# Filler streams that stop at a mark, and transposes that are issued later, in a two-block transformer kernel

## The chip, the cores and the metric

The kernel runs on one core of a Trainium2 chip. The metric is the device time of one execution in microseconds (us), lower is better. One profiled execution gives a trace: every instruction of TensorE (PE; its weight loads, which overlap the products, are PEld), VectorE (DVE), ScalarE (ACT) and GpSimd (POOL), and the transfers (DMA), with start, length and what it waited for.

## The reference

Two blocks of two layers each run on 256 tokens of width 1024, in fp32. Cut to the order of the steps:

```
# first block (h: 256 x 1024)
for i in 0, 1:
    u = rms_norm(h);  y = stick_breaking_attention(u) if i == 0 else dilated_attention(u)
    h += rms_norm(y); u = rms_norm(h)
    h += rms_norm(square(relu(u @ w_ff_in[i])) @ w_ff_out[i])
    h += (p[i] @ w_ple[i]) * sigmoid(rms_norm(h) @ w_ple_gate[i])
# second block: x = h and a context xc of 256 more tokens; shift, scale, gate from a small product
for i in 0, 1:
    hl, hc = modulate(x), modulate(xc)
    oc, ol = mla_pool_mixer(hc, hl) if i == 0 else gqa_mixer(hc, hl)   # layer 1: keys and values of xc only
    x += gate * ol;  x += gate * conv_ffn(modulate(x))
    if i == 0: xc += gate * oc;  xc += gate * conv_ffn(modulate(xc))
return rms_norm(x) * g_final
```

dilated_attention projects to q, k and v of 3 groups of heads, turns q and k by rope, and takes a softmax over masked scores. mla_pool_mixer has low-rank q and k/v paths (cq, ck) and a pooling branch with a product after it. conv_ffn is up, a convolution over three tokens, silu times u, down.

## The kernel before

**Products.** All products keep fp32 accuracy by splitting an operand in a rounded half and its remainder: `mm3` (lines 194 to 197) issues three products for one. A weight block of 512 KB is brought into a stage `ws`, ACT casts it to `wh` (L183) and DVE subtracts that to get `wl` (L184); `put_split` (L200, L201) does the same for activations. Inputs of a product must lie with the feature on the partitions, so normalised tokens go through TensorE transposes (`flip_group`, L231), and heads through others (L786, L813, L833, L837 in the dilated attention, L965 in `heads_T`, L1355 in the gqa mixer). PSUM tiles come from three pools of two buffers each: `acc` (two banks a tile), `mm` (the main path) and `fx` (fillers).

**Stages.** In the profiled execution the stick-breaking attention ends at about 175 us, the first FFN with its ple step at about 475, the dilated attention at about 690, the second FFN and ple at about 960, the latent MLA mixer at about 1130, the first conv FFN at about 1390, the gqa mixer at about 1500, and the last conv FFN at the end.

**Fillers.** The context xc needs nothing of the first block. Its work is a Python generator, `ctx_gen` then `ctx1_gen`, in the queue `ctx`: a norm (`ctx_norm`), `mla_gen` on the context (also used for the latent with main-path tiles), the out projection, a second `ctx_norm`, the context's conv FFN, a third `ctx_norm`. The main path calls `fill(n)` where TensorE would wait: the call adds n to the queue's credit and steps the generator while credit is left. A step yields its price in us of TensorE (negative while it holds open PSUM banks). In the dilated attention, `proj(qr + 1)` is stepped in the same way (queue `main`) between the steps of `attend(qr)`; for the last one, qr = 3, no projection is left and the queue `ctx` fills (`ctx_ok`). The `FILL` table holds the credits. `until_dense(n)` steps the queue until a long product stream lies ahead.

**Order.** These generators set in which order instructions are written. A scheduler then orders each engine's row by its own estimates, and each engine runs its row strictly in order. SyncE issues the weight transfers in its own row.

Of the kernel before, what the change touches and what calls it, by code (L numbers as in the profile page):

```python
# [14 lines left out]
ALU = mybir.AluOpType  # L15
# [4 lines left out]
D = 1024  # L20
# [8 lines left out]
PBUFS = 4  # L29
FILL = dict(sb1=5.0, sb2=1.25, sb3=0.5, sb_end=6.0, sbd=6.0, sbm=0.8, m0=1.0, mix0=8.5, mix1=8.5, f1c=1.6,  # L30
            f1d=8.0, post0=9.6, post1=12.0, dp0=5.6, dp1=8.0, ple0=10.0, ple1=10.0, dl0=3.38, dl1=7.65, dl2=2.4,
# [70 lines left out]
def two_block_kernel(ctx: ExitStack, tc: tile.TileContext, a: dict, out: bass.AP, dbg=None):  # L102
# [139 lines left out]
    def norm_one(src, g, shift, f, tt, bank):  # L242
# [5 lines left out]
        for grp in f.groups:  # L248
# [8 lines left out]
            c0 += w  # L257

    class Feat:

# [54 lines left out]
    dense = [0.0]  # L315

    def fill_step(q):
        try:
            w = next(queues[q][0])
            open_banks[q] = w < 0  # L320
            credit[q] -= abs(w)
        except StopIteration:
            open_banks[q] = False
            queues[q].pop(0)
            if q == "mod":
                credit[q] = 0.0

    def clean(q):
# [3 lines left out]
    def fill(n, q="ctx"):  # L332
        if q in rival:
            clean(rival[q])
        credit[q] += n
        while credit[q] > 0 and queues[q]:
            fill_step(q)
        if not queues[q]:
            credit[q] = 0.0
# [307 lines left out]
    def ffn1(i, u, before_end):  # L647
        w1, w2 = a["w_ff_in"][i], a["w_ff_out"][i]
        G = FF1 // 256
        with tc.tile_pool(name="ff", bufs=2) as p:  # L650
# [35 lines left out]
            for g in range(G):  # L686
                if g + 1 < G:
                    up(g + 1)
                next(gv, None)
                if i == 1:  # L690
                    pass
                elif g < G - 3:
                    fill(FILL["f1c"])
                elif g == G - 3:
                    until_dense(FILL["f1d"])
                if g == G - 2:
                    clean("ctx")
                    for _ in gv:
                        pass
                    before_end()  # L700
                down(g)
                if i == 1:
                    next(gv, None)
        return y

# [39 lines left out]
    def dilated(u):  # L745
        w_in, w_out = a["w_in_dil"][0], a["w_out_dil"][0]
        wv = w_in.rearrange("k (g r n) -> k g r n", g=3, r=3)
        with tc.tile_pool(name="dl", bufs=2) as p:
# [3 lines left out]
            def proj(qr):  # L752
                v = p.tile([128, 2, 3, 128], F32, tag="v", name="v")
                qk = p.tile([128, 3, 512], F32, tag="qk", name="qk")
                for g in range(3):
# [12 lines left out]
                    tok = p.tile([128, 2, 4, 64], F32, tag="tok", name="tok")  # L768
                    for tt in range(2):
# [11 lines left out]
                    vec.tensor_tensor(out=x2, in0=x2, in1=r[1], op=ALU.add)  # L781
                    ps = mm1()
                    for part in range(2):
                        for tt in range(2):
                            c0 = part * 256 + tt * 128
                            pe.transpose(ps[:, c0:c0 + 128],  # L786
                                         tok[:, tt, 2 * part:2 * part + 2, :].rearrange("p n d -> p (n d)"), ident)
# [136 lines left out]
    def mla_gen(u, rope, p, alloc, bank, pair, score_pair, res, prev):  # L924
# [8 lines left out]
        cq = Feat(alloc, 3, "cq")  # L933
        ps = yield from lin_part(u, KC, mla_w["mix0_w_in"], 0, 384, pair)
        for tt in range(2):
            r = rstd(ps[tt][:, 0:384], 384)
            t = tmp((128, 384))
            vec.scalar_tensor_tensor(out=t, in0=ps[tt][:, 0:384], scalar=r, in1=gq, op0=ALU.mult, op1=ALU.mult)
            to_T(t, cq, tt, bank)
        yield 0.01  # L940
        ck = Feat(alloc, 2, "ck", paired=True)
        kr = p.tile([128, 2, 32], F32, tag="kr", name="kr", bufs=1)
        ps = yield from lin_part(u, KC, mla_w["mix0_w_in"], 384, 288, pair)
        for tt in range(2):
            act.copy(out=kr[:, tt, :], in_=ps[tt][:, 256:288])
            r = rstd(ps[tt][:, 0:256], 256)
            t = tmp((128, 256))
            vec.scalar_tensor_tensor(out=t, in0=ps[tt][:, 0:256], scalar=r, in1=gkv, op0=ALU.mult, op1=ALU.mult)
            to_T(t, ck, tt, bank)
            if rope:  # L950
                rope_pairs(kr[:, tt:tt + 1, :], 1, 16, ca_t[:, tt, :], sa_t[:, tt, :], p)
        yield 0.01
        ps = yield from lin_part(u, KC, mla_w["mix0_w_in"], 672, 512, pair)
# [66 lines left out]
        for g2 in range(2):  # L1020
# [10 lines left out]
            dT = tmp((128, 512))  # L1031
            act.copy(out=dT, in_=ps1)
            ps2 = bank()
            for g in range(2):
                pe.matmul(ps2[:, g * 256:(g + 1) * 256], pws[:, 2 * g2 + g, :], dT[:, g * 256:(g + 1) * 256],
                          start=True, stop=True)
            for g in range(2):
# [4 lines left out]
                cat.put(4 + gg, t)  # L1042
            yield 2.7

# [9 lines left out]
    def soft_heads(nh, nk, q, k, v, dv, scale, dst, p, al, bank, score_pair):  # L1054
# [43 lines left out]
        for hd in range(nh):  # L1098
# [7 lines left out]
            flip(hd)  # L1106
            yield 0.5 * nk
            if (hd + 1) % per == 0:
# [80 lines left out]
    def ctx_norm(k, i, m):  # L1189
        g, sft = mod_row(i, 1, m + 1), mod_row(i, 1, m)  # L1190
        u = Feat(c4, KC, "uc")
        for tt in range(2):
            t = c4([128, D], F32, "xc")
            nc.sync.dma_start(out=t, in_=xc_source(k)[tt * 128:(tt + 1) * 128, :])
            norm_one(t, g, sft, u, tt, fx1)
        return u

    def ctx_gen():
        u = ctx_norm(0, 0, 0)
        yield 4.0  # L1200
        res = {}
# [6 lines left out]
        for nh in range(2):  # L1208
            ps = yield from lin_part(cat, 8, mla_w["mix0_w_out"], nh * 512, 512, fx_pair)
            for tt in range(2):  # L1210
# [6 lines left out]
                nc.sync.dma_start(out=xc_d[0][tt * 128:(tt + 1) * 128, sl], in_=t2)  # L1217
        u = ctx_norm(1, 0, 3)
        yield 4.0
        f = [c4([128, D], F32, "fsum") for _ in range(2)]  # L1220
# [74 lines left out]
    def gqa_kv_gen(u, rope, p, al, bank, pair, res):  # L1295
# [6 lines left out]
        for tt in range(2):  # L1302
# [4 lines left out]
            else:  # L1307
# [3 lines left out]
                              op=ALU.mult)  # L1311
        yield 0.01
        ps1 = bank()
# [10 lines left out]
    def ctx1_gen():  # L1324
        u = ctx_norm(2, 1, 0)
        yield 4.0
        stage_done["ctx1n"] = True
        yield from gqa_kv_gen(u, False, fillp, c4, fx1, fx_pair, gctx)

    def gqa(u):  # L1330
        w_in, w_out = a["gqa_w_in_2"][0], a["gqa_w_out_2"][0]
        with tc.tile_pool(name="gq", bufs=2) as p:
# [9 lines left out]
            def proj(hf, pair, bank):  # L1342
# [8 lines left out]
                yield 0.01  # L1351
                for tt in range(2):
# [152 lines left out]
```

## Time and profile before

| | |
|---|---|
| median of 3 runs | 1722.03 us (1718.5 to 1724.54) |
| the profiled execution | 1722.1 us; its span 1720.3 us; granted TensorE clock 0.988 of full |
| TensorE busy | 1635.5 us, 95% of the span, 10259 matmul instructions |
| VectorE, ScalarE busy | 1211.1 us (70%), 926.6 us (54%) |
| DMA | 337.65 MB, 196 GB/s on average |

The span is the trace from first to last instruction; 1.8 us of the time lie outside of it. Matmuls are pipelined: the length of one includes its fill, and the distance of two starts is what a product costs in a stream.

### The profile page before, as it was taken

Reading aid. Unit: us, or ns where it says so; the run is one execution under the profiler, and the core shown is the slowest. Engines: PE = TensorE matmul, PEld = TensorE weight load, DVE = VectorE, ACT = ScalarE, POOL = GpSimd, SP = SyncE. Lnnn points to the kernel's source line nnn. Section 1 sums busy time; section 2 is a strip of 40 time slices with the busy share of each in tenths; the row PEclk is TensorE's granted clock in tenths of the full one; section 3 lists DMA queues with packets and bytes.
Section 4 is the critical chain, followed back from the end, with each engine's and each line's share of the span. In section 5 each row is a group of like instructions: output and inputs, shape, how many; then the busy total and the mean of one; then the engine's idle time right before and its main releaser. Section 6 shows DMA issues by size and latency. Waiting matters only on the chain.

```text
span 1720.3 us, 28310 instructions
## 1 busy us (share of the span) xinstructions
PE 1635.5 (95%) x10259; PEld 1428.7 (83%) x10260; DVE 1211.1 (70%) x2251; ACT 926.6 (54%) x1854; POOL 44.6 (3%) x69
## 2 busy tenths in 40 slices
PE   7998999999999999989989999999999999989997
PEld 6767888887788879877978898888989987779997
DVE  4437777678788886767767866867686687676665
ACT  5536555545655556544446555764555555545554
POOL 0000000000000000000000000000000000000000
PEclk9999999999999999999999999999999999989999
DMA  7777666665766665777876555345776664246662
GB/s 240 259 257 232 203 217 214 207 217 165 241 186 205 185 188 160 242 236 245 280 231 208 176 172 174 115 136 180 233 239 205 185 187 148 72 153 187 186 187 98
DMA packets 301039, 337.65 MB, mean 196 GB/s; under 512 B 18384, under 2 KB 246164, under 8 KB 300900
## 3 DMA queue, kind: packets, MB, share of 16 engines
q1 hardware_dynamic: 300900, 335.86, 62.4%
q8 instruction: 80, 1.31, 0.3%
q14 instruction: 59, 0.48, 0.1%
HBM read 332.56 MB, written 3.23 MB: 195 GB/s over the span
## 4 chain that ended last, share of the span: by engine, by line
PE 55%; DVE 14%; DMA 13%; issue 4%; ACT 3%; SPq 1%; POOL 1%; ACTq 0%; POOLq 0%; DVEq 0%
PE mm L195 6%; PE mm L196 6%; PE mm L197 6%; PE acc L197 6%; PE acc L196 6%; PE acc L195 6%; DMA ws<-in_w_mod 6%; DVE wl L184 5%; PE fx L195 4%; PE fx L196 4%; PE fx L197 4%; DMA ws<-in_w_ff_in 2%; DVE ga L497 2%; DMA ws<-in_w_in_dil 2%; ACT wh L183 1%
## 5 line engine op out<-in xcount | busy, mean ns | idle before, releaser
L184 DVE TENSOR_TENSOR wl<-ws,wh 128x512 fp32r<-128x512 f32 (+1 forms) x1004 | 638.1, 668 | 273.3 <-ACT wh L183 261.5
L183 ACT CAST wh<-ws 128x512 fp32r<-128x512 f32 (+1 forms) x1004 | 568.6, 604 | 477.8 <-PE mm L196 132.7
L197 PE MATMUL mm<-uh,wl 128*128 128x256 f32 x1344 | 382.9, 285 | 8.4 <-DVE wl L184 8.1
L195 PE MATMUL mm<-uh,wh 128*128 128x256 f32 x1344 | 382.3, 284 | 0.3
L196 PE MATMUL mm<-ul,wh 128*128 128x256 f32 x1344 | 381.5, 284 | 0.0
L197 PEld LDWEIGHTS mm<-uh,wl 128*128 128x128 f32 x1344 | 258.6, 192 | 11.5 <-DVE wl L184 11.0
L195 PEld LDWEIGHTS mm<-uh,wh 128*128 128x128 f32 x1344 | 258.7, 193 | 5.0 <-DVE ul L201 0.9
L196 PEld LDWEIGHTS mm<-ul,wh 128*128 128x128 f32 x1344 | 258.7, 193 | 2.6
L195 PE MATMUL acc<-wh,hh 128*128 128x512 f32 x432 | 172.1, 399 | 0.0
L196 PE MATMUL acc<-wl,hh 128*128 128x512 f32 x432 | 171.3, 397 | 0.0
L197 PE MATMUL acc<-wh,hl 128*128 128x512 f32 x432 | 170.2, 394 | 0.0
L497 DVE SCALAR_TENSOR_TENSOR ga<-ws,cst,ga 128x1024 f32<-128x1024 f32 x84 | 106.3, 1281 | 57.7 <-DMA ws<-in_w_mod 57.5
L195 PE MATMUL fx<-uch,wh 128*128 128x256 f32 x352 | 102.2, 290 | 0.0
L197 PE MATMUL fx<-uch,wl 128*128 128x256 f32 x352 | 100.9, 287 | 0.0
L196 PE MATMUL fx<-ucl,wh 128*128 128x256 f32 x352 | 100.5, 286 | 0.0
L197 PEld LDWEIGHTS acc<-wh,hl 128*128 128x128 f32 x432 | 81.9, 190 | 18.9 <-issue 1.2
L195 PEld LDWEIGHTS acc<-wh,hh 128*128 128x128 f32 x432 | 82.2, 190 | 17.6 <-issue 1.6
L196 PEld LDWEIGHTS acc<-wl,hh 128*128 128x128 f32 x432 | 82.3, 191 | 14.5
L195 PE MATMUL mm<-wh,uh 128*128 128x384 f32 (+1 forms) x256 | 85.3, 333 | 1.9 <-ACT wh L183 1.1
L196 PE MATMUL mm<-wl,uh 128*128 128x384 f32 (+1 forms) x256 | 83.0, 324 | 0.3 <-DVE wl L184 0.3
L197 PE MATMUL mm<-wh,ul 128*128 128x384 f32 (+1 forms) x256 | 82.0, 322 | 0.0
L217 POOL TENSOR_TENSOR s<-s,neghalf 128x1 f32<-128x1 f32 (+2 forms) x52 | 39.9, 767 | 1452.9 <-DVE s L215 1413.1
(405 smaller groups left out, 2705.8 us busy)
## 6 DMA issues: line engine op xcount, KB each, us to landing
ws<-in_ffn_w_up SPq DMA_DIRECT2D x528, 128.0 KB
ws<-in_w_mod SPq DMA_DIRECT2D x96, 512.0 KB
ws<-in_ffn_w_down SPq DMA_DIRECT2D x66, 512.0 KB
ws<-in_w_ff_in SPq DMA_DIRECT2D x64, 512.0 KB
ws<-in_w_ff_out SPq DMA_DIRECT2D x64, 512.0 KB
ws<-in_w_in_dil SPq DMA_DIRECT2D x96, 192.0 KB
ws<-in_w_in_sb SPq DMA_DIRECT2D x24, 512.0 KB
row<-mod SPq DMA_DIRECT2D x19, 512.0 KB
```

The source lines that it names most:

```text
L183: act.copy(out=h[:, s], in_=st[:, s])
L184: vec.tensor_sub(out=l[:, s], in0=st[:, s], in1=f32(h[:, s]))
L195: pe.matmul(o, lh, rh, start=start, stop=False)
L196: pe.matmul(o, lh, rl, start=False, stop=False)
L197: pe.matmul(o, ll, rh, start=False, stop=stop)
L217: gp.tensor_tensor(out=r, in0=v, in1=neghalf.to_broadcast([128, w]), op=ALU.pow)
L497: vec.scalar_tensor_tensor(out=o, in0=st, scalar=c, in1=o, op0=ALU.mult, op1=ALU.add)
```

## The change

A step of a generator can now yield a `Pause`, which is a number like the others; where `fill` meets one, it drops the credit that is left, so that the rest of this call issues nothing more from that queue. Steps whose next instruction needs the result of another engine yield one. The norm of the context becomes a generator too (`norm_tok` works in place at full width, where `norm_one` went by halves). In `mla_gen` the norms of cq and ck are made for both token tiles ahead of the Pause, and the transposes follow it. The product after the pooling (L1035) and the head transposes (L965) get a Pause ahead of them. In the dilated projection the q/k transposes of a group of heads are issued by `flip` after the second weight block of the next group, and use an `fx` bank. In the gqa mixer the k/v stream goes to its Pause first, then the q stream, and both are then drained. In the first FFN the fill of 1.6 per group becomes two of 0.8.

```
-            f1c=1.6,
+            f1c=0.8,
...
+    def norm_tok(t, g, shift):
+        r = rstd(t, D)
+        vec.tensor_mul(out=t, in0=t, in1=g)
+        vec.scalar_tensor_tensor(out=t, in0=t, scalar=r, in1=shift, op0=ALU.mult, op1=ALU.add)
...
+    class Pause(float):
+        pass
     def fill_step(q):
+        w = 0.0
...
+        return isinstance(w, Pause)
...
         while credit[q] > 0 and queues[q]:
-            fill_step(q)
+            if fill_step(q):
+                credit[q] = min(credit[q], 0.0)
...
                 down(g)
                 if i == 1:
                     next(gv, None)
+                elif g < G - 3:
+                    fill(FILL["f1c"])
...  # dilated, proj
                         yield -1.95
+                        if kb == 1 and g - 1 in toks:
+                            flip(g - 1)
+                            yield -0.45
...
-                    ps = mm1()
-                    for part in range(2): ...
-                    act.copy(out=qk[:, g, :], in_=ps)
-                    yield 0.5
+                    toks[g] = tok
+                    yield Pause(0.05)
+                flip(2)
                 keep[qr] = (v, qk)
+                yield 0.5
...  # mla_gen, cq (ck alike)
         for tt in range(2):
             r = rstd(ps[tt][:, 0:384], 384)
-            t = tmp((128, 384))
-            vec.scalar_tensor_tensor(out=t, ...)
-            to_T(t, cq, tt, bank)
-        yield 0.01
+            vec.scalar_tensor_tensor(out=ct[:, tt], ...)
+        yield Pause(2.0)
+        for tt in range(2):
+            to_T(ct[:, tt], cq, tt, bank)
+        yield Pause(1.0)
...
+            yield Pause(1.0)
             heads_T([qtok[:, 0], qtok[:, 1]], qT[hf], act)
-            yield 1.0
+            yield Pause(1.0)
...
             act.copy(out=dT, in_=ps1)
+            yield Pause(1.5)
             ps2 = bank()
...
-            yield 2.7
+            yield Pause(1.2)
...  # soft_heads
-            yield 0.5 * nk
+            yield Pause(0.5 * nk)
...  # ctx_norm
-            norm_one(t, g, sft, u, tt, fx1)
+            norm_tok(t, g, sft)
+            yield Pause(0.1)
+            to_T(t, u, tt, fx1)
+            yield Pause(2.0)
...  # ctx_gen (three places)
-        u = ctx_norm(0, 0, 0)
-        yield 4.0
+        u = yield from ctx_norm(0, 0, 0)
...  # gqa: two steps before transposes yield Pause(0.01) for 0.01, and
-            queues["main"].extend([g0, kvg])
-            while lat.get("kT") is None:
-                fill_step("main")
+            for g in (kvg, g0):
+                while not isinstance(next(g), Pause):
+                    pass
+            queues["main"].extend([kvg, g0])
             drain_main()
```

How the rows of TensorE move is seen at three places. Beside the first FFN, the context's pooling: its first product (L1029, after the change L1059) and the second one (L1035, after L1066), which reads `t`, ACT's copy of the first one's result. `acc<-wh,hh` are the FFN's down products, `mm<-uh,wh` its up products. Before:

```order
L1029 MATMUL fx<-ws,pt 128x256 x4
L195 MATMUL acc<-wh,hh 128x512
L196 MATMUL acc<-wl,hh 128x512
L197 MATMUL acc<-wh,hl 128x512
L195 MATMUL acc<-wh,hh 128x512
L1035 MATMUL fx<-t_3482,ws 128x256 x2
```

After (the lines left out are 64 more of the FFN's products):

```order
L1059 MATMUL fx<-ws,pt 128x256 x4
L195 MATMUL mm<-uh,wh 128x256
L196 MATMUL mm<-ul,wh 128x256
L197 MATMUL mm<-uh,wl 128x256
...
L196 MATMUL acc<-wl,hh 128x512
L197 MATMUL acc<-wh,hl 128x512
L195 MATMUL acc<-wh,hh 128x512
L196 MATMUL acc<-wl,hh 128x512
L197 MATMUL acc<-wh,hl 128x512
L1066 MATMUL fx<-t_3631,ws 128x256 x2
```

Four products stood between the two, and now 72 do.

In the dilated attention, the transposes of a projected group (tok) at one of twelve places. `mm<-wh,uh 128x384` are the projection's products; L833 and L837 (after: L858 and L862) are transposes of the softmax. Before, the group's transposes stand ahead of the next group's first product:

```order
L818 MATMUL acc<-dm_96,ident_b 128x256
L833 MATMUL fx<-ident,P 128x128 x3
L837 MATMUL fx<-ident,P 128x128 x3
L786 MATMUL mm<-ident,tok 128x128 x4
L195 MATMUL mm<-wh,uh 128x384
L196 MATMUL mm<-wl,uh 128x384
```

After:

```order
L858 MATMUL fx<-ident,P 128x128 x3
L862 MATMUL fx<-ident,P 128x128 x3
L195 MATMUL mm<-wh,uh 128x384
L196 MATMUL mm<-wl,uh 128x384
L197 MATMUL mm<-wh,ul 128x384
L195 MATMUL mm<-wh,uh 128x384
L777 MATMUL fx<-ident,tok 128x128 x4
L196 MATMUL mm<-wl,uh 128x384
```

They now stand inside the products of the next group.

In the last dilated attention (qr = 3): `acc<-qk` are scores, `mm<-ident,P` transposes of probabilities, `mm<-PT,v` the products with v, `fx<-uch,wh` products of the context stream, `fx<-ident,xc` its norm's transposes. Before, the piece from the end of the first scores to the second scores:

```order
L802 MATMUL acc<-qk 128x128 x2
...
L196 MATMUL fx<-ucl,wh 128x256
L197 MATMUL fx<-uch,wl 128x256
L813 MATMUL mm<-ident,P 128x128 x3
L195 MATMUL fx<-uch,wh 128x256
L196 MATMUL fx<-ucl,wh 128x256
...
L818 MATMUL acc<-dm_96,ident_b 128x256
L822 MATMUL acc<-qk 128x256 x3
```

After, from the end of the first scores to the products of the context:

```order
L827 MATMUL acc<-qk 128x128 x2
L231 MATMUL fx<-ident,xc 128x128 x8
L847 MATMUL acc<-qk 128x256
L838 MATMUL mm<-ident,P 128x128 x3
...
L847 MATMUL acc<-qk 128x256 x3
L838 MATMUL mm<-ident,P 128x128 x3
L858 MATMUL mm<-ident,P 128x128 x3
L862 MATMUL mm<-ident,P 128x128 x3
...
L874 MATMUL mm<-PT_6756,v 64x256
...
L231 MATMUL fx<-ident,xc 128x128 x8
L195 MATMUL fx<-uch,wh 128x256
```

Before, context products stand between the steps of this attention; after, the only context work inside it is one group of 8 transposes, and 144 context products come behind it and behind a second group. On VectorE the norm of that second group stands behind the last copy of the attention's probabilities (`PT`):

```order
L757 TENSOR_SCALAR P<-P,s 128x768
L859 COPY PT_6757<-mm 128x3x128
L215 TENSOR_SCALAR s<-s 128x1
L262 TENSOR_TENSOR xc<-xc,row 128x1024
L263 SCALAR_TENSOR_TENSOR xc<-xc,s,row 128x1024
L201 TENSOR_TENSOR o<-mm,o 128x256
L201 TENSOR_TENSOR ucl<-fx,uch 128x4x128 x2
```

Before, the norm of that stage (L245) was done ahead of this attention.

## Rows read from the trace of the kernel before

**Rows 1.** Waits of TensorE: line, what it waited for: us in total, times, longest.
```profile
PE mm L786 <- DVE tok L780: 4.8, 4, 1.6
...
PE mm L1035 <- ACT t L1032: 3.3, 2, 2.0
...
PE fx L231 <- DVE t L254: 2.6, 5, 0.7
PE fx L1035 <- ACT t L1032: 2.4, 1, 2.4
...
PE fx L231 <- DVE s L215: 2.1, 1, 2.1
...
PE fx L195 <- ACT qT L968: 2.0, 1, 2.0
...
PE mm L1355 <- DVE qt L1293: 1.4, 2, 0.7
...
PE fx L965 <- ACT qtok L977: 1.2, 1, 1.2
```

**Rows 2.** Three windows: length; busy PE, PEld, DVE, ACT, POOL; granted clock, DMA share, GB/s.
```profile
350.00:375.00 25.00, 22.65 (x124) 19.64 (x123) 17.54 (x26) 11.63 (x22) 0.00 (x0) 0.93 0.71 228
625.00:650.00 25.00, 23.77 (x151) 19.28 (x149) 20.06 (x43) 11.27 (x28) 0.53 (x1) 0.93 0.69 205
1050.00:1075.00 25.00, 21.70 (x130) 19.14 (x129) 13.77 (x28) 12.06 (x23) 0.00 (x0) 0.93 0.64 189
```

**Rows 3.** ACT's timeline at the second pooling product: start, length, [idle before, releaser].
```profile
1064.25 0.62 ACT L183 CAST wh<-ws 128x512 fp32r<-128x512 f32 x1 [0.68 <-DMA ws<-in_ffn_w_up]
...
1065.62 0.62 ACT L183 CAST wh<-ws 128x512 fp32r<-128x512 f32 x1 [0.29 <-DMA ws<-in_ffn_w_up]
1066.14 0.58 ACT L1032 COPY t<-mm 128x512 f32<-128x512 f32 x1
```

**Rows 4.** PE's timeline in two undisturbed streams: start, length.
```profile
1165.05 0.39 PE L195 MATMUL acc<-wh,cat 128*128 128x512 f32 x1
1165.28 0.39 PE L196 MATMUL acc<-wl,cat 128*128 128x512 f32 x1
```
```profile
669.55 0.28 PE L195 MATMUL fx<-uch,wh 128*128 128x256 f32 x1
669.67 0.28 PE L196 MATMUL fx<-ucl,wh 128*128 128x256 f32 x1
```

**Rows 5.** Groups by form, 480 to 700 us: count | busy, mean ns | idle before.
```profile
L195 PE MATMUL mm<-wh,uh 128*128 128x384 f32 x192 | 66.9, 349 | 0.9 <-ACT qk L788 0.8
...
L770 ACT COPY tok<-mm 128x256 f32<-128x256 f32 x24 | 9.0, 373 | 2.7 <-PE mm L197 2.7
...
L771 ACT COPY v<-mm 128x128 f32<-128x128 f32 x24 | 6.6, 275 | 0.0
```

**Rows 6.** The same view, the softmax and the norm of the context.
```profile
L736 DVE TENSOR_REDUCE s<-acc 128x1 f32<-128x768 f32 x8 | 7.5, 941 | 0.0
L740 ACT ACTIVATE P<-acc,s 128x768 f32<-128x768 f32 x8 | 7.2, 905 | 10.6 <-DVE s L738 10.5
...
L743 DVE TENSOR_SCALAR P<-P,s 128x768 f32<-128x768 f32 x8 | 4.9, 614 | 0.0
...
L740 ACT ACTIVATE P<-acc,s 128x384 f32<-128x384 f32 x8 | 4.7, 581 | 4.8 <-DVE s L738 4.7
...
L834 DVE COPY PT<-fx 128x384 f32<-128x384 f32 x6 | 3.3, 552 | 0.0
...
L245 DVE TENSOR_TENSOR t<-xc,row 128x1024 f32<-128x1024 f32 x2 | 2.5, 1226 | 1.8 <-DMA ws<-in_w_in_dil 1.4 <-DMA xc<-xc 0.4
```

**Rows 7.** PE's timeline in the last dilated attention: transposes ahead of the last scores, product with v.
```profile
641.29 0.63 PE L786 MATMUL mm<-ident,tok 128*128 128x128 f32 x4 [1.16 <-DVE tok L780]
...
666.64 2.17 PE L849 MATMUL mm<-PT,v 128*64 128x256 f32 x24
```

**Rows 8.** ACT's timeline at the end of the stick-breaking attention.
```profile
156.81 0.62 ACT L183 CAST wh<-ws 128x512 fp32r<-128x512 f32 x1 [2.35 <-DMA ws<-in_w_out_sb]
```

More of the change, by code (lines that the diff above doesn't have):

```diff
@@ L29 @@
 PBUFS = 4
-FILL = dict(sb1=5.0, sb2=1.25, sb3=0.5, sb_end=6.0, sbd=6.0, sbm=0.8, m0=1.0, mix0=8.5, mix1=8.5, f1c=1.6,
+FILL = dict(sb1=5.0, sb2=1.25, sb3=0.5, sb_end=6.0, sbd=6.0, sbm=0.8, m0=1.0, mix0=8.5, mix1=8.5, f1c=0.8,
             f1d=8.0, post0=9.6, post1=12.0, dp0=5.6, dp1=8.0, ple0=10.0, ple1=10.0, dl0=3.38, dl1=7.65, dl2=2.4,
@@ L754, in proj, with flip @@
                 qk = p.tile([128, 3, 512], F32, tag="qk", name="qk")
+                toks = {}
+                def flip(g):
+                    tok = toks.pop(g)
+                    ps = fx1()
+                    for part in range(2):
+                        for tt in range(2):
+                            c0 = part * 256 + tt * 128
+                            pe.transpose(ps[:, c0:c0 + 128],
+                                         tok[:, tt, 2 * part:2 * part + 2, :].rearrange("p n d -> p (n d)"), ident)
+                    act.copy(out=qk[:, g, :], in_=ps)
                 for g in range(3):
@@ L781, in proj @@
                     vec.tensor_tensor(out=x2, in0=x2, in1=r[1], op=ALU.add)
-                    ps = mm1()
[L783 to L787, printed above, removed]
-                    act.copy(out=qk[:, g, :], in_=ps)
-                    yield 0.5
+                    toks[g] = tok
+                    yield Pause(0.05)
+                flip(2)
                 keep[qr] = (v, qk)
+                yield 0.5
             def attend(qr, bank):
@@ L934, in mla_gen @@
         ps = yield from lin_part(u, KC, mla_w["mix0_w_in"], 0, 384, pair)
+        ct = al([128, 2, 384], "ct")
         for tt in range(2):
             r = rstd(ps[tt][:, 0:384], 384)
-            t = tmp((128, 384))
-            vec.scalar_tensor_tensor(out=t, in0=ps[tt][:, 0:384], scalar=r, in1=gq, op0=ALU.mult, op1=ALU.mult)
-            to_T(t, cq, tt, bank)
-        yield 0.01
+            vec.scalar_tensor_tensor(out=ct[:, tt], in0=ps[tt][:, 0:384], scalar=r, in1=gq, op0=ALU.mult, op1=ALU.mult)
+        yield Pause(2.0)
+        for tt in range(2):
+            to_T(ct[:, tt], cq, tt, bank)
+        yield Pause(1.0)
         ck = Feat(alloc, 2, "ck", paired=True)
@@ L946, in mla_gen @@
             r = rstd(ps[tt][:, 0:256], 256)
-            t = tmp((128, 256))
-            vec.scalar_tensor_tensor(out=t, in0=ps[tt][:, 0:256], scalar=r, in1=gkv, op0=ALU.mult, op1=ALU.mult)
-            to_T(t, ck, tt, bank)
+            vec.scalar_tensor_tensor(out=ct[:, tt, 0:256], in0=ps[tt][:, 0:256], scalar=r, in1=gkv, op0=ALU.mult,
+                                     op1=ALU.mult)
             if rope:
                 rope_pairs(kr[:, tt:tt + 1, :], 1, 16, ca_t[:, tt, :], sa_t[:, tt, :], p)
-        yield 0.01
+        yield Pause(2.0)
+        for tt in range(2):
+            to_T(ct[:, tt, 0:256], ck, tt, bank)
+        yield Pause(1.0)
         ps = yield from lin_part(u, KC, mla_w["mix0_w_in"], 672, 512, pair)
@@ L980, in mla_gen @@
             qT.append(al([96, 4, T], "qT"))
+            yield Pause(1.0)
             heads_T([qtok[:, 0], qtok[:, 1]], qT[hf], act)
-            yield 1.0
+            yield Pause(1.0)
         kT = [al([96, 4, T], "kT") for _ in range(2)]
@@ L1194, in ctx_norm @@
             nc.sync.dma_start(out=t, in_=xc_source(k)[tt * 128:(tt + 1) * 128, :])
-            norm_one(t, g, sft, u, tt, fx1)
+            norm_tok(t, g, sft)
+            yield Pause(0.1)
+            to_T(t, u, tt, fx1)
+            yield Pause(2.0)
         return u
     def ctx_gen():
-        u = ctx_norm(0, 0, 0)
-        yield 4.0
+        u = yield from ctx_norm(0, 0, 0)
         res = {}
@@ L1217, in ctx_gen @@
                 nc.sync.dma_start(out=xc_d[0][tt * 128:(tt + 1) * 128, sl], in_=t2)
-        u = ctx_norm(1, 0, 3)
-        yield 4.0
+        u = yield from ctx_norm(1, 0, 3)
         f = [c4([128, D], F32, "fsum") for _ in range(2)]
@@ L1311, in gqa_kv_gen @@
                               op=ALU.mult)
-        yield 0.01
+        yield Pause(0.01)
         ps1 = bank()
@@ L1324, in ctx1_gen @@
     def ctx1_gen():
-        u = ctx_norm(2, 1, 0)
-        yield 4.0
+        u = yield from ctx_norm(2, 1, 0)
         stage_done["ctx1n"] = True
@@ L1350, in proj @@
                     gain_rope(qt_[:, tt], ps[tt], 4, tt, q_tables)
-                yield 0.01
+                yield Pause(0.01)
                 for tt in range(2):
```

## The prediction

> **What bounds the kernel now.** The table comes first: TensorE is busy 95% of the span, in every stage, so a microsecond is saved only where TensorE stands idle or runs at a lower clock. Next I read the waits of TensorE [rows 1], since each says what came last and how long it cost; then the windows around the longest ones, for the clock [rows 2]; then the timeline of ACT at one of them, to see why the awaited instruction was late [rows 3]. Three things are to be seen.
>
> First, the waits that the change aims at are small and few: the group transposes of the dilated projection 4.8 us in four, the second pooling product 3.3 in two on the main path and 2.4 in one in the filler, a norm of the context 2.6 in five, a wait on a norm at the end of the stick attention 2.1, the filler's ck product behind a head copy 2.0, the gqa transposes 1.4, the filler's head transposes 1.2 [rows 1]. Together 19.8 us, 1.1% of the span.
>
> Second, after a long wait the granted clock falls to half for a while: in three windows of 25 us it is 0.93 [rows 2], so 0.07 x 25 = 1.75 us are lost in each, beside the idle time.
>
> Third, why the copies are late. The second pooling product waits for ACT's copy of the first one's result. That copy takes 0.58, but stands behind two casts of weights, each of which had waited for its transfer [rows 3]. So the awaited instruction is late because ACT's row holds it behind a cast that waits for DMA; more products ahead of the transposes help, if these have their weights.
>
> A product in a stream costs the distance of starts: 0.23 us for 512 columns, 0.12 for 256 [rows 4].
>
> **The change part by part.** The sum is made against the profiled execution, 1722.1 us, which is the median of the three runs to 0.1 us.
>
> T1, the filler beside the first FFN. The pooling product (2.4), the ck product (2.0) and the head transposes (1.2) [rows 1] get a Pause ahead of them, so the rest of the filler's turn is dropped and the FFN's products come in between: 72 at the pooling product, 48 of 256 columns and 24 of 512, 48 x 0.12 + 24 x 0.23 = 11.3 us [rows 4] against a copy of 0.58 behind at most a cast or two of 0.62 [rows 3]. The waits go: 5.6. With them goes the half clock in 350 to 375 us, 1.75 [rows 2]. The context's attention heads are cut in smaller pieces by the same Pauses; their PV products may wait more, 0 to 0.7 us by the nearest row, the head transposes' wait of 1.2 [rows 1], so I take 0.4. T1 = 5.6 + 1.75 - 0.4 = **+7.0** (bounds +3 to +8).
>
> T2, the latent's MLA stage. Of the two main-path waits of the pooling product one is 2.0 and the other 3.3 - 2.0 = 1.3 [rows 1]. At the first site the order after has only six products of 0.12 in between, 0.7 us, less than the casts ahead of the copy, so 1.3 stays; at the second it has 42, 5.0 us, so 2.0 goes, and with it the half clock in 1050 to 1075 [rows 2]: T2 = 2.0 + 1.75 = **+3.8**. The cq transposes lose some products ahead of them and the ck ones gain some; I book 0, with 1.3 either way by the wait that stays.
>
> T3, the dilated projection. Four of the twelve group transposes waited, 4.8 us [rows 1]. After the change they stand inside the next group's products, with half a group, 24 products of 0.16 (384 columns at the pitch of rows 4, an estimate), in front; the rope's six short DVE steps are long done. The last one, 1.16 at 641 us [rows 7], has no next group and stays. T3 = 4.8 - 1.2 = **+3.6**. The upper bound is 6, the 4.8 and the clock that one of them may cost; the lower is under the rivals (D).
>
> T4, the context's norms: 2.6 us in five waits of its transposes on the norm [rows 1]. The Pause between norm and transposes puts main-path work there: **+2.6** (bounds 0 to 2.6). The in-place norm multiplies 1024 columns once and then needs one more instruction of that width, where halves let the first transposes start earlier; DVE is free for that in those stages.
>
> T5, the end of the stick attention (2.1, [rows 1]). There ACT's exponent stands behind a cast that waited 2.35 for the weights of the out projection [rows 8]; the Pause at the head's end moves filler, not that transfer. **0** (bounds -2 to +4: SyncE issues some small transfers of the filler ahead of that weight, or the wait and a clock loss of 1.75 go).
>
> T6, gqa (1.4 in two). The k/v stream goes first, then the q stream, and one stream's products still cover the other's rope. **0** (bounds -1.5 to +1.4).
>
> T7, the loss: the last dilated attention. Before, context products filled it: from the group's transposes at 641.29 to the product with v at 666.64 [rows 7] TensorE had no gap of note. After, the context stream arrives there at its second norm, whose Pauses end each turn, and the order shows what is left: eight transposes of xc, and 144 context products only behind the product with v and behind another eight transposes, whose norm stands on VectorE behind the last copy of the probabilities. So TensorE has to wait out the softmax. Counted from the end of the first scores, with the durations of [rows 6] and short steps of 0.15 to 0.2 estimated for maximum, sum and reciprocal: first softmax, two heads one after the other (reduce some 0.55, half the long one; exponent 0.58; scale 0.41) 3.0, transposes and copies of 0.55 each, second scores from 4.1 to 6.0 (they also wait for an acc tile); second softmax, reduce 0.94, exponent 0.91, scale 0.61, for two heads overlapped, to 10.2; transposes and copies, product with v from 11.5 to 12.5; then the norm's multiplication of 1.23 and a second instruction of the same width, to 13.9 (the multiplication beside the last transposes); transposes and split, first context product at 15.0. TensorE's own work in these 15 us is about 6 (the second scores, 24 transposes, 24 products with v). Idle: 9. Around such idle time the clock falls, by [rows 2] 1.75 a time; I take two, 3.5, less the 1.75 that 625 to 650 us loses already [rows 2]. T7 = -(9.1 + 3.5 - 1.75) = **-10.9** (bounds -6, if the steps overlap better and the clock costs nothing more, to -14, if the norm waits for its row of gains too). The 48 context products that no longer fit come later, in other fills, at no price.
>
> The split of the FFN's fill in two of 0.8 adds no work; its effect is in T1's order.
>
> Sum: 7.0 + 3.8 + 3.6 + 2.6 + 0 + 0 - 10.9 = +6.1. Forecast 1722.1 - 6.1 = **1716.0 us**.
>
> **The rivals.** A is the sum as made: 1716.0, its own range 1711 to 1720.
>
> B, the last attention is cheaper: the scheduler's row leaves 9 us idle by my count, but the two heads' chains may overlap, and context weights fetched early let their products start at once. At T7 = -5 the time is 1722.1 - 17.0 + 5 = 1710. For it: DVE and ACT have little else there when no filler runs. Against: the second norm stands behind the last copy whatever the overlap.
>
> C, half of the gains arrive: the stretches are paced by the casts that wait for DMA [rows 3], so a removed wait partly comes back as one on a weight. (17.0 / 2) - 10.9 = -2.4, 1724.5.
>
> D, PSUM. The next group of the dilated projection needs both mm banks, which are free only after the four copies of the group before (tok 0.37 and v 0.28, two each: 1.3 us [rows 5]). Before, the transposes stood there and used the same pool; after, the next group's products run into the copies at once. Twelve groups at up to 0.8 is 9.6 in the worst case; where softmax work stands in between, as in most of the orders, nothing. At T3 = -5 the time is 1722.1 + 8.6 - 6.1 = 1724.6. The Trainium skill ("Perfetto Trace Analysis", section Optimization Strategy) says that a gap that repeats on the engine that should be full can mean that PSUM lacks room for the next tile; by that the four alike waits would be of this sort, and moving the transposes would not end them. The trace names the rope on DVE as their releaser.
>
> E, the other side: transfers set the pace. A half block of weights arrives every 1065.62 - 1064.25 = 1.37 us [rows 3], a block in 2.74, and the 24 products that use it take 24 x 0.12 = 2.88 [rows 4]. The margin is 5%. If the filler's products that move up bring their transfers with them and a block takes over 2.88, TensorE gains nothing from the waits removed in T1, T2 and T3, and keeps T7: 2.6 - 10.9 = -8.3, 1730.4. Against it: the other stretches have a DMA share of 0.7 [rows 2], not 1.
>
> **How the numbers follow.** Chances: A 0.48, B 0.20, C 0.14, D 0.06, E 0.12. The time is A's. The range is 1704 to 1726: down to B with the upper bounds of T3 and T5 in part, up to C and D; outside lie E and some 0.05 at the low end. A change of this kernel under 0.3%, 5.2 us, can't be told from none. Faster means below 1716.9: B and 0.28 of A, 0.48. Slower means above 1727.2: E and a little of C, 0.13. The rest, 0.39, is within.
>
> **What would show it.** In the changed kernel's waits of TensorE, the pooling product beside the first FFN, the ck product, the head transposes, three of the four group transposes and the context's norm should be gone (T1 to T4), the granted clock at 350 to 375 us should be 1.0, and one pooling wait of about 1.3 should be left on the main path. In the last dilated attention the timeline should show waits of TensorE on softmax steps and on the xc norm, some 9 us in all, a clock below 0.9 around them, and 144 context products behind. I am wrong if that attention is filled from elsewhere, if waits of products on `wl` or `wh` grow by what the others lose (C, E), or if the projection's first products wait on the copies of tok and v (D).

## The result, and the profile after

The changed kernel takes 1729.52 us (median of 11 runs, 1723.38 to 1736.72), the one before 1719.59 in 11 runs beside it: ratio 1.0061, interval 1.0039 to 1.0083. It is 10 us slower, where 6 us faster was forecast. The profiled execution after took 1736.72 us, its span 1734.9, granted clock 0.979. It is the slowest of its 11 runs, as e7's below is of its 6, while those of e12 and e14 are the fastest of their 12, so times are compared by the ratios and traces show where the time goes.

The waits of TensorE after, in the columns of [rows 1]:

```profile
PE fx L777 <- DVE tok L809: 4.2, 3, 2.0
PE fx L195 <- DVE fsum L1279: 3.6, 3, 1.9
PE fx L1094 <- DVE t L1071: 3.6, 1, 3.6
...
PE fx L231 <- DVE xc L263: 2.5, 2, 2.2
PE mm L858 <- DVE s L752: 2.2, 1, 2.2
...
PE mm L1105 <- DVE P L757: 1.6, 1, 1.6
PE mm L1105 <- DVE s L752: 1.4, 1, 1.4
PE mm L1066 <- ACT t L1062: 1.2, 1, 1.2
PE mm L838 <- DVE s L752: 1.2, 1, 1.2
...
PE mm L195 <- ACT v L800: 0.8, 2, 0.5
```

Every wait that the change aimed at in the context's mixer (L1035, the ck product, L965 in [rows 1]) is gone, and one pooling wait is left on the main path, 1.2. But the list is as long as before: scores on a scaled copy (L1094 on L1071, 3.6 at once), the down products of the context's FFN on its sums (fsum), softmax steps (L858, L838, L1105), norms (xc). And three group transposes still wait, 4.2 in place of the 4.8 of [rows 1], where T3 left one of 1.2.

Windows after, in the columns of [rows 2]; the first holds the wait on L1071, the next two the last dilated attention, the last the MLA heads:

```profile
375.00:400.00 25.00, 21.39 (x107) 18.23 (x106) 18.19 (x35) 11.02 (x23) 0.00 (x0) 0.86 0.70 228
1075.00:1100.00 25.00, 22.03 (x137) 20.23 (x137) 17.52 (x43) 16.73 (x33) 0.00 (x0) 0.86 0.54 168
```
```profile
625.00:650.00 25.00, 20.99 (x113) 15.47 (x111) 19.78 (x46) 12.00 (x28) 0.53 (x1) 0.90 0.73 227
650.00:675.00 25.00, 21.69 (x160) 19.53 (x161) 14.17 (x27) 11.81 (x22) 1.46 (x1) 0.83 0.32 99
```

The low clock moved with the waits: from 350 to 375 us to 375 to 400, from 1050 to 1075 to 1075 to 1100, and there it costs 0.14 x 25 = 3.5 us each where 1.75 was lost in [rows 2]. In the last attention 0.10 x 25 + 0.17 x 25 = 6.75 us go, which is 13.5 us at half clock; TensorE stood idle for some of that time.

The last attention after, on TensorE:

```profile
640.73 0.49 PE L827 MATMUL acc<-qk 64*128 64x128 f32 x4 [0.28 <-ACT qk L779]
641.16 1.09 PE L231 MATMUL fx<-ident,xc 128*128 128x128 f32 x8
...
644.06 0.55 PE L838 MATMUL mm<-ident,P 128*128 128x128 f32 x3 [1.19 <-DVE s L752]
...
651.51 0.87 PE L858 MATMUL mm<-ident,P 128*128 128x128 f32 x3 [2.19 <-DVE s L752]
...
655.37 3.69 PE L874 MATMUL mm<-PT,v 128*64 128x256 f32 x24
658.99 1.09 PE L231 MATMUL fx<-ident,xc 128*128 128x128 f32 x8
661.05 0.39 PE L195 MATMUL fx<-uch,wh 128*128 128x256 f32 x1 [0.96 <-DVE ucl L201]
```

From the first scores to the first context product TensorE waits on the softmax and the norm; the 24 products with v take 3.69 where 2.17 did [rows 7], at half clock.

**Excess by stage.** To compare whole stages I use one number worked out from the trace: for every two successive matmuls the distance of their starts, less the mean distance that the same form has in kernel before (of distances under 1.6 times its median), summed over a stage. It holds idle time and what a low clock costs, and not the filler work that lands in a stage. The stages are cut at the main path's norms (before: 198, 442, 692, 953, 1178, 1402, 1517 us; a cut at 480, behind the first ple step, moves no entry by more than 0.6).

```
                     before  after   e7    e13   e14   e12
stick attention        46.7   48.8  45.0  47.5  46.2  46.4
first FFN              19.0   20.1  23.8  22.7  18.3  17.0
dilated attention      24.9   30.3  38.0  26.1  23.3  21.5
second FFN             24.6   23.0  22.4  23.8  22.0  21.0
MLA mixer              20.6   23.3  22.0  22.9  18.6  19.3
conv FFN               3.5    7.4   4.0   5.0   4.8   4.1
gqa                    29.3   28.9  27.7  28.3  30.7  30.0
last conv FFN          4.6    5.3   5.5   5.9   5.1   5.6
```

These are single executions. How far they scatter is seen where kernels are the same: up to the end of the first FFN e2's instructions on TensorE, VectorE and ScalarE come in the same order as those of the kernel before, and its excess there is 22.6 against 19.0; seven kernels with the order of the changed one (after, e3 to e6, e9, e10) read 17 to 21 there. So a difference under 4 us says little. After against before stands out in the dilated attention alone (+5.4), and no stage gains what was forecast.

### The profile page after: what moved, and what is told of

Its sections match the earlier page's. It is cut to its first block, busy times and chain, and to the rows that moved or that the text cites. A ratio compares the mean times of both kernels' runs of the same rounds, so it can differ in the third digit from the quotient of the medians.

```text
span 1734.9 us, 28313 instructions
## 1 busy us (share of the span) xinstructions
PE 1647.8 (95%) x10260; PEld 1438.4 (83%) x10260; DVE 1208.8 (70%) x2245; ACT 921.4 (53%) x1852; POOL 47.8 (3%) x69
## 4 chain that ended last, share of the span: by engine, by line
PE 63%; DMA 15%; DVE 13%; ACT 3%; issue 3%; SPq 2%; POOL 1%; ACTq 0%; DVEq 0%; POOLq 0%
PE mm L195 8%; DMA ws<-in_w_mod 8%; PE mm L196 8%; PE mm L197 8%; PE acc L197 6%; PE acc L195 6%; PE acc L196 6%; DVE wl L184 4%; PE fx L195 3%; PE fx L196 3%; PE fx L197 3%; DVE ga L509 2%; DMA ws<-in_w_ff_in 2%; DMA ws<-in_w_ff_out 2%; DMA ws<-in_ffn_w_up 1%
```

## The experiments

Each ratio is to runs of the kernel before on the same chip, with its 95% interval. The first four ask whether the loss sits in the dropped credit, in one place, or in the reordering.

**e1**, the changed kernel without the drop:

```
-        return isinstance(w, Pause)
+        return False
```

> The changed kernel, but fill keeps its credit at a Pause, so a Pause is only a price again; the reordering by flip, ctx_norm, mla_gen and gqa stays. Theory 1, the loss is one place (the last dilated attention loses its filler): the context products come back there, and the time falls by the whole loss there, 6 to 11 us from 1729.5, to 1719 to 1723; the other stages keep their excess of the changed kernel. Theory 2, each dropped credit uncovers work somewhere (stick end, the MLA heads at 1083, the conv FFN at 1187 to 1222): all of these shrink too, and the time is at or below that of before, 1715 to 1719. Theory 3, the loss is in the reordering, not in the dropped credit: it stays above 1726.

Measured: 1735.2 us, 1.0075 (1.0054 to 1.0096). As theory 3 has it, the drop of credit is not the cause. The last attention is no better, the windows 625 to 650 and 650 to 675 us have a clock of 0.77 and 0.69.

**e2**, before with the new projection (flip) alone; its diff is the dilated part of the change's.

> The kernel before with the dilated projection's transposes moved by flip, nothing else. T3 as predicted: 3.6 us faster than before (ratio 0.998), stage 481 to 692 us with 3 to 4 us less idle. The PSUM rival D: the next group's products wait on the copies of tok and v, and the time is 0 to 5 us slower than before.

Measured: 1726.22 us, 1.0026 (1.0003 to 1.0049): slower, as rival D has it, and against T3. D's own wait, of the next products on the copies of v, is 2.2 us in two. The largest wait in its profile is at the last group, which has no next one: the transposes waited 3.51 us at 646.69. ACT's row shows why:

```profile
642.95 0.62 ACT L183 CAST wh<-ws 128x512 fp32r<-128x512 f32 x1 [0.87 <-DMA ws<-in_ffn_w_up]
644.28 0.62 ACT L183 CAST wh<-ws 128x512 fp32r<-128x512 f32 x1 [0.71 <-DMA ws<-in_ffn_w_up]
644.80 0.36 ACT L785 COPY tok<-mm 128x256 f32<-128x256 f32 x1
```

The copies of tok stand behind casts of the filler's weights, each of which waits for its transfer.

**e3**, the changed kernel, no drop in the last attention alone:

```
-            if fill_step(q):
+            if fill_step(q) and hold[0]:
...
+                hold[0] = qr < 3
```

> The changed kernel, but in the last dilated attention alone the credit is not dropped at a Pause. 148 context products then stand between the softmax steps again. Theory 1: nearly the whole difference to before goes, time 1718 to 1722. Theory 2: only this place's 5 to 6 us go (the stage between the first FFN's end and the dilated attention's end has 5.4 us more excess than before), time 1723 to 1725.

Measured: 1733.15 us, 1.007 (1.0047 to 1.0094). Nothing came back, though 148 context products stand inside the attention: they stand behind the transposes of the second xc half, which waited 5.5 us on VectorE's softmax steps at 650. So the products are not what is missing, but the norm ahead of them.

**e4**, the changed kernel with the dilated projection of before:

> The changed kernel with the dilated projection of before (no flip). T3 as predicted: 3.6 us slower than the changed kernel, about 1733. Rival D: 0 to 5 us faster than it, 1725 to 1729. If the last dilated attention changes with it (the order has to say), its part is read from the excess of that stage.

Measured: 1737.45 us, 1.0088 (1.0062 to 1.0113), 0.27% slower than the changed kernel. By that flip helps here by 4.6 us, about T3, but the two intervals overlap.

**Where the context got late.** e1 and e3 sent me to the trace for the norm itself. VectorE's first instruction of the second norm, before and after (count, first and last start us):

```profile
L245 DVE TENSOR_TENSOR t<-xc,row x2: 1226/1226/1226, 504.1 to 516.9; 128x1024 f32<-128x1024 f32 x2
```
```profile
L262 DVE TENSOR_TENSOR xc<-xc,row x2: 1216/1216/1217, 507.7 to 655.3; 128x1024 f32<-128x1024 f32 x2
```

Before, both token tiles were normed at 504 and 517; after, the second one waits until 655. The code says why. Ahead of the dilated attention's loop `clean("ctx")` steps the context until no PSUM bank is open:

```
    def clean(q):
        while open_banks[q]:
            fill_step(q)
```

The step that closes the out projection's banks ran on, in the kernel before, through the whole of `ctx_norm` up to `yield 4.0`. As a generator of small steps it stops after the norm of the first tile, and the queue `ctx` is next served in the last attention, over 130 us later. This is theory 4, which the next runs test.

**e5**, the changed kernel, the context stepped through its norm ahead of the stage (the entry n1 is set behind the second `ctx_norm`):

```
             fill(FILL["ple0"])
+            clean("mod")
+            while "n1" not in stage_done:
+                fill_step("ctx")
```

> The changed kernel, and the context stream is stepped through its second norm ahead of the dilated attention, so its products fill the last attention as before. Theory 4 (the norm cut into steps lets clean stop behind its first half, so the context is one norm late for a whole stage): the excess of the dilated stage falls from 30 to 25 us or less, the clock there is low for at most 3.4 us, and the time falls by 6 to 10 us from 1729.5, to 1720 to 1724. Theory 5 (flip makes the next group's products wait on the copies of tok and v, which costs as much as it saves): the stage stays at 28 or above.

Measured: 1720.44 us, 0.9989 (0.997 to 1.0007). The dilated stage's excess is 21.5, and the clock never falls in it: theory 4.

**e6**, e5 with the projection of before:

> As e5, with the dilated projection of before. Theory 5: faster than e5 by about 4 us, the stage's excess at 25. T3 as predicted: slower than e5 by 3.6 us.

Measured: 1734.46 us, 1.0064 (1.0038 to 1.009). This pair does not measure flip: in e6 the xc transposes came early and waited 6.1 us on the norm at 498, which e5's order avoids.

**e7**, the kernel before, only the norm cut into steps:

```
-            norm_one(t, g, sft, u, tt, fx1)
+            norm_tok(t, g, sft)
+            yield 0.1
+            to_T(t, u, tt, fx1)
+            yield 2.0
```

> The kernel before, with only the context's norm as a generator of small steps (plain numbers, no dropped credit, nothing else moved). Theory 4: this alone makes the context late, the order has eight transposes and no context product until behind the second scores of the last attention, the stage's excess rises from 25 to 32 or more, and the kernel is 8 to 14 us slower than before, ratio 1.005 to 1.008. The rival (the loss needs the dropped credit or the Pauses of mla_gen): within 3 us of before.

Measured: 1736.26 us, 1.0078 (1.0049 to 1.0106). Theory 4 holds with one edit and no Pause. (The edit also takes the full-width norm of the change; e5 keeps that and loses nothing.) Its windows show more low clock than the changed kernel's:

```profile
625.00:650.00 25.00, 21.30 (x136) 17.66 (x135) 20.64 (x41) 12.97 (x30) 0.53 (x1) 0.93 0.70 208
650.00:675.00 25.00, 21.10 (x113) 17.34 (x113) 13.18 (x28) 9.64 (x19) 1.46 (x1) 0.66 0.46 139
```

**e8**, before with the new `mla_gen`, its Pauses and the drop, and the context stepped as in e5:

> The kernel before, with mla_gen, the head and pooling Pauses and the dropped credit, and the context stepped through its second norm ahead of the dilated attention (which before does by itself). T1 and T2 as predicted: 10.8 us faster than before, ratio 0.994. Theory 2, the dropped credit uncovers other places (the scores behind the pooling at 394, the MLA heads at 1087): the gains are given back, within 3 us of before.

Measured: 1733.36 us, 1.0059 (1.0032 to 1.0085). Not clean: the stepping put a wait of 3.5 us of its own on the xc transposes at 502. e13 repeats it without.

**e9**, as e5, but the loop stands at `clean("ctx")`, where before did the norm:

> The changed kernel, and the context is stepped through its second norm at the place where before did it (behind the first projection of the dilated attention). Theory 4 again, without the norm ahead of the stage as in e5: 1719 to 1722, the dilated stage's excess 21 to 25 us.

Measured: 1724.1 us, 1.0012 (0.9992 to 1.0033); the dilated stage's excess 22.1. 8 us of the loss are gone, as theory 4 says.

**e10**, e9 with the projection of before:

> e9 with the dilated projection of before. T3 as predicted: 3.6 us slower than e9, the stage's excess 3 to 4 us higher. If e6's 14 us over e5 were flip's, it is 10 us or more slower; if the copies of tok and v cost what flip saves (theory 5), it is within 2 us of e9.

Measured: 1724.86 us, 1.0017 (0.9996 to 1.0037), 0.05% slower than e9; the stage's excess 28.2, 6 above e9 in this execution, which the medians don't bear out.

**e11**, e9 with another credit:

```
-            f1c=0.8,
+            f1c=1.2,
```

> e9 with the first FFN's fills at 1.2 for 0.8, so that the last pooling product and the first scores of the context come out in the fills, with 48 products between them, and not in until_dense, which doesn't stop at a Pause. Theory 6, the wait of the scores on the pooling's scaled copy (3.8 us at 393.7 after the change, with a half clock of 6.8 us) took the place of the waits that T1 removes: it goes, the excess of the first FFN's stage falls from 20 to 15 us or less, and the time is 5 us below e9. If the stage is paced by weights, products wait on wl in its place and the time is within 2 us of e9.

Measured: 1725.76 us, 1.0021 (1.0003 to 1.0038), no better than e9. The wait of the scores on L1071 went, but the first FFN's excess is 23.7: transposes of probabilities wait in their place, 3.1 and 1.3 us, and the pooling product 3.5. The waits change place again.

**e12**, the changed kernel with the norm of before, as one step, and its three calls of before:

```
-            norm_tok(t, g, sft)
-            yield Pause(0.1)
-            to_T(t, u, tt, fx1)
-            yield Pause(2.0)
+            norm_one(t, g, sft, u, tt, fx1)
...
-        u = yield from ctx_norm(1, 0, 3)
+        u = ctx_norm(1, 0, 3)
+        yield 4.0
```

> The changed kernel with the context's norm of before (one step, by halves); all else stays. Theory 4: the whole of the slip is in the norm's steps, so this is as e9, 1719 to 1722, with the last attention filled. T4 as predicted (the Pause between norm and transposes is worth 2.6): 2.6 us slower than e9.

Measured: 1719.33 us, 0.999 (0.997 to 1.001), 12 us below the changed kernel. The last attention's windows are as full as before's, at full clock:

```profile
625.00:650.00 25.00, 23.70 (x164) 20.49 (x165) 21.26 (x46) 13.39 (x29) 0.53 (x1) 1.00 0.68 203
650.00:675.00 25.00, 25.00 (x190) 23.04 (x189) 16.97 (x34) 15.84 (x31) 0.00 (x0) 1.00 0.56 179
```

**e13**, before with the new `mla_gen`, its Pauses and the drop, nothing else:

> The kernel before with mla_gen, the head and pooling Pauses and the dropped credit, nothing else; the context's norm is one step as before, so it isn't late (e8 stepped it early and put a wait of 3.6 us on it at 502). T1 and T2 as predicted: 10.8 us faster than before, ratio 0.994. If the waits only change their place (the scores at 390 behind the pooling's scaled copy, products on wl, the pooling product at 1068): within 3 us of before.

Measured: 1726.34 us, 1.003 (1.0011 to 1.0049): slower, where T1 and T2 have it 10.8 us faster.

**e14**, e12 with the projection of before:

> e12 with the dilated projection of before: a second pair for flip, beside e9 and e10. T3 as predicted: 3.6 us slower than e12, ratio to before 1.001. If flip is worth nothing on the whole: within 2 us of e12.

Measured: 1725.39 us, 1.0016 (0.9998 to 1.0035), 0.26% or 4.5 us slower than e12.

## Why the prediction was wrong, step by step

Four of the kernels make a chain in which each adds one part to the one ahead, so the ratios split the loss:

```
before -> e13   mla_gen, Pauses, drop       1.0000 -> 1.0030   +5 us   (T1 + T2: -10.8 predicted)
e13 -> e14      gqa order, FFN fill split   1.0030 -> 1.0016   -2 us   (T6 and the split: 0)
e14 -> e12      flip                        1.0016 -> 0.9990   -4.5 us (T3: -3.6)
e12 -> after    norm in steps               0.9990 -> 1.0061  +12 us   (T4: -2.6, T7: +10.9)
```

Each ratio is uncertain by 0.2% or so, 3 to 4 us, so the difference of two by some 5. The first step is a single ratio, 1.9 to 8.4 us by its interval, and the last is clear of 5; the two between are not. The split also holds for this order of the parts alone: flip on the kernel before (e2) costs 4.5 us.

**T7 was right in place and near in size, wrong in its cause.** The change to the norm costs 12 us, and the last attention is where it shows: of pairs that differ in whether the context is in time, the dilated stage's excess rises by 8.2 (e9 to after), 8.8 (e12 to after), 11.2 (e10 to e4) and 13.1 (before to e7). After, the waits there add up to 0.28 + 1.19 + 2.19 + 0.96 and two shorter ones of 0.22 and 0.83, 5.7 us, where I had 9.1. The half clock lasts 13.5 us in one stretch; TensorE stood idle for 3.0 of them (2.19 and 0.83), so the rest costs about 5.3, less the 1.75 of before, where I had 1.75 net. Together that is some 9.2 against 10.9: the two errors go opposite ways, so that the size came out near is in part luck. The cause that I gave, Pauses that end each turn of the filler, was not it: e1 takes the drop away and loses as much, e7 has no Pause at all and loses 13 us. It is the cut of one step in four, which lets `clean` stop between them.

**T1 and T2 failed: the step "The waits go: 5.6", and the 2.0 of T2 in the same way.** The named waits of T1 did go, but the time didn't. The prediction covered the producer's next consumer and didn't ask what that instruction's own successor would wait for. In e13, the part by itself, all waits of TensorE in the first FFN (200 to 448 us) add up to 8.5 us; in the kernel before (198 to 442) they are 7.8, and 9.0 in e2, whose order is the same there. These two are most of e13's:

```profile
PE fx L1075 <- DVE t L1052: 4.6, 1, 4.6
PE mm L197 <- DVE wl L184: 2.7, 3, 1.4
```

The excess of that stage says the same: 22.7 in e13 and 20.1 in e8, which have one order there, against 19.0 and 22.6 in before and e2. So the waits of T1 came back as others and the stage neither gained nor lost; in which stage e13's 5 us go can't be read from single executions. In e13, and after, the scores behind the second pooling product wait for an fx bank. After:

```profile
387.05 1.03 PE L1066 MATMUL fx<-t,ws 128*128 128x256 f32 x4
387.91 1.03 PE L1094 MATMUL fx<-kT,qT 96*128 96x256 f32 x4
388.59 0.59 PE L195 MATMUL acc<-wh,hh 128*128 128x512 f32 x1
...
393.72 1.65 PE L1094 MATMUL fx<-kT,qT 96*128 96x256 f32 x3 [3.61 <-DVE t L1071]
```
```profile
389.31 1.29 DVE L184 TENSOR_TENSOR wl<-ws,wh 128x512 fp32r<-128x512 f32 x2 [1.29 <-ACT wh L183]
391.58 0.69 DVE L184 TENSOR_TENSOR wl<-ws,wh 128x512 fp32r<-128x512 f32 x1 [0.98 <-ACT wh L183]
...
392.79 0.87 DVE L1071 TENSOR_SCALAR t<-fx,pscale 128x256 f32<-128x256 f32 x2
```

The product at 387.05 leaves a bank that VectorE must empty (L1071) before the scores at 393.72 may write; that copy stands behind subtractions for weights that wait for ACT's casts, which wait for transfers. The same wait is 4.65 in e13, 2.7 in e12. It comes in a stretch which `until_dense` steps through, and that loop doesn't stop at a Pause: the context, with the new prices of the steps in `mla_gen`, is later than before and does its last pooling there (at 387, where it was at 367). That it is the fx bank is read from the order and the pool's two buffers; e11 moved the place and the wait became others. In the same stage products waited on `wl` where none did before, 1.3 in two after (0.96 of it at 290.40) and 2.7 in e13. In the MLA stage the pooling wait that stays was right after (1.2 against 1.3), though it is 2.5 in e13, where all waits of that stage are 9.0 against 7.2 before; and new ones came after: 1.9 on fsum at 1187.02, 1.39 and 1.58 on softmax steps at 1087.16 and 1089.37. Rival C said half of the gains; in e13 none is left. The split of the FFN's fill in two, which I booked at nothing, may be worth some 4 us there: up to the end of the first FFN e12 and e14 differ from e8 and e13 in it alone, and read 17.0 and 18.3 against 20.1 and 22.7. The prediction's own third point, that an awaited copy is late because ACT's row holds it behind a cast that waits for DMA, holds for every next instruction too, and I used it for the named waits of T2 and T5 alone. What in e13 brings this about, the dropped credit or the new order in `mla_gen`, was not run apart.

**T4** came out at its lower bound, 0, as far as the runs tell. The norm's waits are 2.5 us in two after, for 2.6 in five. e12 has the norm in one step and the context in time, 0.999; with steps and the context in time e9 has 1.0012 and e5 0.9989.

**T3** stays open. By the ratios e14 to e12 gives 4.5 us and e4 to after 4.6, but e10 to e9 gives 0.8 and e2, flip alone, lost 4.5; each is uncertain by 4 to 5. The waits don't bear its mechanism out. Those of the group transposes and of the products behind them, added up, go from 6.2 (before) to 7.1 (e2), from 5.8 (e10) to 5.6 (e9), from 6.0 (e14) to 4.5 (e12) and from 10.2 (e4) to 5.0 (after). (The 24 products in front of the transposes I priced at 0.16; by [rows 4] 384 columns take 0.17 to 0.18, which changes nothing.) Rival D's wait is real: in e12 the next group's products wait on the copies of v three times,

```profile
PE mm L195 <- ACT v L800: 3.3, 3, 1.4
```

and its mechanism is the copies' place behind other work on ACT, at 503:

```profile
501.48 1.06 ACT L223 ACTIVATE junk<-xc 128x1024 bf16<-128x1024 f32 x1 [1.74 <-DMA xc<-xc]
...
502.54 0.91 ACT L183 CAST wh<-ws 128x512 fp32r<-128x512 f32 x2
503.36 0.36 ACT L799 COPY tok<-mm 128x256 f32<-128x256 f32 x1
503.62 0.26 ACT L800 COPY v<-mm 128x128 f32<-128x128 f32 x1
```

The Trainium skill's sentence on gaps that repeat ("Perfetto Trace Analysis", section Optimization Strategy) fits that wait, 3.3 us in all, though not the ones that flip was to remove. Whether flip loses on the kernel before and gains on others stays open: the one profile of e2 shows 3.5 us at the last group, but no run moves that alone.

**T5, T6** were booked at 0, and no run tells otherwise, since none has them alone. **E** put the time at 1730.4, within a us of what came, and its outcome, that removed waits give nothing, is what T1 and T2 showed, but its mechanism was not seen: the DMA share beside the first FFN is 0.70 in 375 to 400 us after, where it was 0.71 in 350 to 375 [rows 2]. Of its signs one came in part, the longer waits on `wl`. So its time is near in part by luck.

No kernel of the study is faster than before by more than its interval; e12 (0.997 to 1.001) and e5 (0.997 to 1.0007) are the best.

## What to carry to other kernels

A step of a cooperative stream is also the grain at which others stop it: before one is cut, look for every loop that steps it until a condition holds, and ask where the stream would now be left standing, and when it is next served. A removed wait on an in-order engine counts only if the next instruction that shares its bank or its engine's row is ready too; where casts wait for transfers in every stage, book removed waits at little, not whole. A split of a change in a chain of kernels, each with one part more, finds the large parts; here two of the four steps were clear of the scatter.

## What the runs showed of the hardware

What a wait costs in clock is not a fixed price. In the windows of [rows 2] the longest waits are 2.4, 1.2 and 2.0 us, and each window lost 1.75 us, at 0.93 of full. The wait of the scores on L1071 (L1073 in e9) in the first FFN, in two kernels whose order is the same up to there, is 3.6 after and 2.9 in e9; after, the window 375 to 400 us ran at 0.86, and in e9 at full clock:

```profile
375.00:400.00 25.00, 21.48 (x129) 18.91 (x128) 20.48 (x41) 12.37 (x29) 0.00 (x0) 1.00 0.68 212
```

In the last attention of e7, where TensorE waits 2.75 us on the softmax in a stretch of small products, the window 650 to 675 us ran at 0.66, which is 17 us at half clock (1.2 GHz), some 4 of them idle, and the dense context products that followed were still at half speed:

```profile
659.34 1.97 PE L231 MATMUL fx<-ident,xc 128*128 128x128 f32 x8 [2.75 <-DVE s L744]
...
662.97 0.41 PE L195 MATMUL fx<-uch,wh 128*128 128x256 f32 x1
663.18 0.41 PE L196 MATMUL fx<-ucl,wh 128*128 128x256 f32 x1
```

Their starts are 0.21 us apart, where the same products are 0.12 apart at 669 us in the kernel before [rows 4].
